# Stick-breaking attention on one core: scores and transposes as separate steps, ScalarE's norms and sigmoids in fixed groups, the mask as float32r

## The chip, the cores and the metric

The kernel runs on one core of one Trainium2 chip. The metric is the device time of one execution in microseconds (us); the kernel before has a median of 2329.46 us over 3 runs (2329.19 to 2330.55). The engines are named as in the profile: PE is TensorE, PEld its weight loads, DVE is VectorE, ACT is ScalarE, POOL is GpSimd, SP is SyncE, which issues the transfers of the weights.

## The reference, cut to what matters

A trunk of four residual layers on 512 tokens of width 1024: pooling, SSD, attention, pooling, each followed by a SwiGLU feed-forward layer. Only the third layer's mixer, the attention, is touched:

```
qkv = (h @ w_qkv).reshape(b, s, 3, 16, 64)
q = rms_norm(qkv[:, :, 0], q_norm);  k = rms_norm(qkv[:, :, 1], k_norm)
z = (q @ k.T) / sqrt(64)                       # per head, strictly causal mask
log_1m = where(mask, log_sigmoid(-z), 0)
after  = reverse cumulative sum of log_1m, without the element itself
a = where(mask, exp(log_sigmoid(z) + after), 0)
o = a @ v;   x = x + o @ w_out
```

The kernel computes the products of `1 - sigmoid(z)` directly, by a scan, and not through logarithms.

## The kernel before

Everything is kept transposed, with the model's width on the 128 partitions and the 512 tokens along a row. A projection (`proj`, `gemm`, L215 to L217) multiplies eight 128x128 weight blocks; each float32 operand is split into a float32r part and a rest, so that each block takes three matmuls of 512 columns. The weights' split (a cast on ACT at L108, a subtraction on DVE at L109) runs four pieces ahead of the matmuls that use them.

Attention works on eight pairs of heads. `ATT_STEPS`, a list of steps, gives the order in which the program is written: `p` is `pair` (two projections q and k, 48 matmuls; the norm of each; the splits of q and k per head), `v` is `values` (96 matmuls of 256 columns, for four heads), `a` is `attend`, `o` is the output projection of two pairs (48 matmuls). A scheduler then places each engine's instructions by data and buffer dependences. It may take them out of program order, but at run time each engine executes its list strictly in order.

A norm (`normal`) is a square on ACT (L781), a split of it (L220, L221), two matmuls that sum over a head's 64 rows (L246, L247), then `rsqrt`: Ln, Exp and Square on ACT (L232, L233, L235) and two steps on DVE (L236, L237). Ln and Exp need one set of ACT's tables, Sigmoid another. An instruction whose set is not loaded gets a table load ahead of it, which carries the line of that instruction. In `pair` the norms ask for no load themselves (`load=False`).

`attend` calls `head` for two heads; `head` takes three pieces of the score matrix (512, 512 and 256 columns; `PIECES`). For each piece `piece` writes z into one of the two PSUM banks `m` (L839; at L844 a matmul of an identity with `never`, both bf16, adds the mask), runs two sigmoids on ACT (c at L846, a at L847), the scan on DVE (L851) and a product (L857). `head` at once transposes the result (L875, PSUM banks `y` and `n`) and copies it to `at` (L877, ACT and DVE in turn). When both heads are done, 24 matmuls weight the values (L888) into the one bank `s`, which the norms' sums use too, and `split` writes the pair's output (two buffers with the tag `o`).

Of the kernel before, what the change touches and what calls it, by code (L numbers as in the profile page):

```python
# [3 lines left out]

# [7 lines left out]
F32R = mybir.dt.float32r  # L12
BF16 = mybir.dt.bfloat16
AF = mybir.ActivationFunctionType
# [3 lines left out]
P = 128  # L18
# [109 lines left out]
def _steps(order, **names):  # L128
    return [(names[s[0]], int(s[1:])) for s in order.split()]
# [6 lines left out]
    x="front", z="gate", d="steps", s="scan", o="out",  # L136
)

ATT_STEPS = _steps(
    "p0 p1 v0 a0 p2 v1 a1 p3 a2 v2 p4 a3 o0 p5 v3 a4 p6 a5 p7 a6 o1 a7 o2 o3",  # L140
    p="pair", v="values", a="attend", o="out",
)

SSD_BUFS = dict(u=2, state=3, f=11, a=6, w=6, o=8, c=2, d=5, sel=1)
ATT_BUFS = dict(kk=4, qq=4, ql=4, p=2, v=12, c=2, a=2, e=2, at=3, o=8)


class Trunk:
# [74 lines left out]
    def rsqrt(self, out, ss, n, load=True):  # L223

        nc = self.nc
        y, q = self.t(), self.t()
        out = y if out is None else out
        if load:
            self.tc.keep_in_program_order(
                nc.scalar.preload_act_table_set("natural_log_exp_and_others")  # L230
            )
        nc.scalar.activation(y, ss, AF.Ln, bias=self.eps, scale=1.0 / n)  # L232
        nc.scalar.activation(y, y, AF.Exp, scale=-0.5)  # L233

        nc.scalar.activation(q, y, AF.Square, scale=math.sqrt(0.5 / n))  # L235
        nc.vector.scalar_tensor_tensor(q, ss, n * EPS, q, op0=ALU.add, op1=ALU.mult)  # L236
        nc.vector.scalar_tensor_tensor(  # L237
            out, q, 1.5, y, op0=ALU.subtract, op1=ALU.mult, reverse0=True
        )
        return out  # L240
# [499 lines left out]


    def attention(self, j, nxt):
        nc = self.nc
        mm = nc.tensor.matmul
        V = nc.vector
        with self.phase("att", **ATT_BUFS) as tl:
            st = self.t((P, P))
# [5 lines left out]
            qg = tl("qg", (P, 1))  # L753
            V.tensor_scalar(qg, self.col("q_norm", 0), 1.0 / math.sqrt(HD), None, op0=ALU.mult)
            kg = self.col("k_norm", 0)
            identb = tl("identb", (P, P), BF16)
            V.tensor_copy(identb, self.ident)

            st = self.t((P, P))
            nc.gpsimd.memset(st, 0.0)  # L760
# [1 line left out]
                out=st, in_=st, pattern=[[-1, P]], base=0, channel_multiplier=1,  # L762
                compare_op=ALU.is_gt, fill=-(2.0**100),
            )
            never = tl("never", (P, P), BF16)
            V.tensor_copy(never, st)
            rcol = tl("rcol", (P, NB))
            zero = tl("zero", (P, 1))
# [4 lines left out]
            def project(q):  # L773
                ps = self.ps("g")
                self.proj(ps)
                V.tensor_tensor(q, ps, self.rstd, op=ALU.mult)
                return q

            def normal(q, gain):
                sq = self.t()  # L780
                nc.scalar.activation(sq, q, AF.Square)  # L781
                pss = self.ps("s")
                self.sums(pss, bd, sq)
                r = self.rsqrt(None, pss, HD, load=False)
                V.scalar_tensor_tensor(q, q, gain, r, op0=ALU.mult, op1=ALU.mult)

            def values(n):
# [13 lines left out]
                    vt.append(v)  # L801
                return vt

            def pair():


                q = project(tl("p"))
                k = project(tl("p"))
                normal(q, qg)
                normal(k, kg)  # L810
                heads = []
                for h in range(2):
                    own = slice(h * HD, (h + 1) * HD)
                    other = slice((1 - h) * HD, (2 - h) * HD)
                    qq, ql, kk = (tl(t, dt=F32R) for t in ("qq", "ql", "kk"))
                    nc.scalar.copy(qq[own], q[own])
                    nc.gpsimd.tensor_copy(qq[other], qq[own])
                    V.tensor_tensor(ql[own], q[own], qq[own].bitcast(F32), op=ALU.subtract)
                    nc.gpsimd.tensor_copy(ql[other], ql[own])
                    nc.scalar.copy(kk[own], k[own])  # L820
                    V.tensor_tensor(kk[other], k[own], kk[own].bitcast(F32), op=ALU.subtract)
                    heads.append((qq, ql, kk))
                return heads


            PIECES = ((0, 2), (3,), (1,))
            FIRST = {0: 0, 2: 1, 3: 4, 1: 8}

            def piece(parts, qbs):


                qq, ql, kk = parts
                n = sum(qb + 1 for qb in qbs) * P
                z = self.ps(next(zs), (P, n))
                at = 0
                for qb in qbs:
                    w = (qb + 1) * P
                    for q in (qq, ql):
                        mm(  # L839
                            z[:, at : at + w], q[:, qb * P : (qb + 1) * P], kk[:, :w],  # L840
                            start=at == 0 and q is qq, stop=False,
                        )
                    at += w
                    mm(z[:, at - P : at], identb, never, start=False, stop=qb == qbs[-1])  # L844
                c, a, e = (tl(t, (P, n)) for t in "cae")
                nc.scalar.activation(c, z, AF.Sigmoid, scale=-1.0)  # L846
                nc.scalar.activation(a, z, AF.Sigmoid)  # L847
                at = 0
                for qb in qbs:
                    w = (qb + 1) * P  # L850
                    V.tensor_tensor_scan(  # L851
                        back(e, at, w), back(c, at, w), zero.to_broadcast([P, w]), 1.0,
                        op0=ALU.mult, op1=ALU.add,
                    )
                    at += w

                V.tensor_tensor(a[:, : n - 1], a[:, : n - 1], e[:, 1:], op=ALU.mult)  # L857
                return a

            def back(t, at, n):  # L860

                (ps, pn), (s, _) = t.ap
                return bass.AP(t.tensor, t.offset + s * (at + n - 1), [[ps, pn], [-s, n]])

            copies = itertools.cycle((nc.scalar.copy, V.tensor_copy))

            def head(parts):

                at = tl("at", (P, 10, P))
                for qbs in PIECES:  # L870
                    a = piece(parts, qbs)
                    n = a.shape[1] // P
                    pt = self.ps(next(ts), (P, n, P))
                    for i in range(n):
                        nc.tensor.transpose(pt[:, i], a[:, i * P : (i + 1) * P], self.ident)  # L875
                    f = FIRST[qbs[0]]
                    next(copies)(at[:, f : f + n], pt)  # L877
                return at

            def attend(f, heads, vt):  # L880
                po = self.ps("s")
                ats = [head(heads[h]) for h in range(2)]

                todo = [(0, 0, 2), (0, 2, 4), (1, 2, 4), (2, 2, 4), (1, 1, 2), (3, 3, 4)]
                for i, (kb, lo, hi) in enumerate(todo):
                    b0, b1 = FIRST[lo] + kb, FIRST[hi - 1] + kb
                    for h in range(2):
                        mm(  # L888
                            po[h * HD : (h + 1) * HD, lo * P : hi * P].rearrange(
                                "p (b t) -> p b t", t=P  # L890
                            ),
                            vt[kb][:, (2 * f + h) * HD : (2 * f + h + 1) * HD],
                            ats[h][:, b0 : b1 + 1 : max(b1 - b0, 1)],
                            start=i == 0, stop=i == len(todo) - 1,
                        )
                hi, lo = tl("o", dt=F32R), tl("o", dt=F32R)
                self.split(po, hi, lo)
                return hi, lo
# [5 lines left out]
                    nc.tensor.transpose(pt, self.rstd[:, b * P : (b + 1) * P], self.ident)  # L904
                    V.tensor_copy(rcol[:, b : b + 1], pt[:, :1])

            qk, vals, os = {}, {}, {}
            for step, n in ATT_STEPS:
                if (step, n) == ("values", 0):
                    rstd_columns()  # L910
                if step == "values":
                    vals[n] = values(n)
                elif step == "pair":
                    qk[n] = pair()
                elif step == "attend":
                    os[n] = attend(n % 2, qk.pop(n), vals[n // 2])
                else:
                    last = n == SB_HEADS // 4 - 1
                    self.out_proj([os.pop(2 * n), os.pop(2 * n + 1)], 4, nxt, last, "ggy")
# [24 lines left out]
def _plan(subs, pool_in, pool_group, ssd_in, ssd_out, sb_qkv, sb_out, gate, up, down):  # L944
# [10 lines left out]
    for sub in subs:  # L955
# [43 lines left out]
        else:  # L999
            j = sub[2]  # L1000
            for step, n in ATT_STEPS:
                if step == "values":
# [100 lines left out]
```

## Time and profile before

| | |
|---|---|
| time of the profiled execution | 2327.25 us |
| its span (first to last instruction) | 2325.5 us |
| median of three runs | 2329.46 us |
| PE busy | 2279.9 us (98%) |
| DVE busy | 1368.6 us (59%) |
| ACT busy | 1011.4 us (43%) |
| mean granted clock of PE | 0.994 |

The span runs from the first to the last instruction; 1.75 us of the profiled execution lie around it. Busy time is the time in which an engine has an instruction running by the records; PE's ends are modelled, so that short stops between matmuls can be hidden in it. Attention takes 316.8 us of the span, from 1230.5 us (first matmul of its first projection) to 1547.3 us, where its last output projection is interleaved with the first one of the feed-forward layer.

### The profile page before, as it was taken

How to read it: one execution, taken by the hardware profiler on the slowest of the kernel's cores; microseconds unless marked ns; L12 is line 12 of the kernel's file. 1: busy time of each engine (PE TensorE's matmuls, PEld its weight loads, DVE VectorE, ACT ScalarE, POOL GpSimd, SP SyncE). 2: the span in 40 equal slices, each digit the busy share in tenths (PEclk: the TensorE clock that was granted, in tenths of full speed). 3: DMA queues.
4: the chain of work that ended last, by engine and by line, in shares of the span. 5: the costliest groups of instructions: out<-in, count | busy, mean ns of one | idle time of the engine just before them, and what ended most of it. 6: DMA issues, size and time to landing. Idle time of an engine off the chain costs nothing.

```text
span 2325.5 us, 26443 instructions
## 1 busy us (share of the span) xinstructions
PE 2279.9 (98%) x10650; PEld 1849.0 (80%) x10650; DVE 1368.6 (59%) x1889; ACT 1011.4 (43%) x1446; POOL 39.6 (2%) x132
## 2 busy tenths in 40 slices
PE   8999999999999999999999988899999999999999
PEld 7888888777777778888888766578888888888887
DVE  8744434778787785444457667884344469534443
ACT  5522223576565763222236777852222244422221
POOL 0000000000000000000001001100000000000000
PEclk9999999999999999999999989999999999999999
DMA  4323222322222223232223112022232232333231
GB/s 160 115 91 109 91 92 74 109 73 73 73 90 74 73 77 105 91 107 93 91 82 100 46 37 82 19 86 96 91 106 94 82 103 88 109 101 99 91 99 65
DMA packets 211898, 205.43 MB, mean 88 GB/s; under 512 B 4800, under 2 KB 204608, under 8 KB 211776
## 3 DMA queue, kind: packets, MB, share of 16 engines
q1 hardware_dynamic: 211632, 203.57, 27.0%
q8 instruction: 84, 1.38, 0.2%
q14 instruction: 38, 0.31, 0.0%
q10 hardware_dynamic: 144, 0.17, 0.0%
HBM read 201.63 MB, written 2.10 MB: 88 GB/s over the span
## 4 chain that ended last, share of the span: by engine, by line
PE 87%; ACT 5%; DVE 5%; issue 1%; DMA 1%; SPq 0%; POOL 0%; DVEq 0%; ACTq 0%; POOLq 0%
PE ps L215 27%; PE ps L216 27%; PE ps L217 27%; PE ps L673 1%; PE ps L888 1%; DVE e L851 1%; DVE wl L109 1%; ACT L233 1%; ACT wh L108 1%; PE ps L679 1%; ACT L232 1%; PE ps L875 0%; PE ps L642 0%; DVE a L857 0%; DMA raw<-in_pool_in_dram 0%
## 5 line engine op out<-in xcount | busy, mean ns | idle before, releaser
L108 ACT CAST wh<-raw 128x1024 fp32r<-128x1024 f32 (+3 forms) x394 | 402.7, 1023 | 1070.1 <-PE ps L216 850.1
L215 PE MATMUL ps<-xh,wh 128*128 128x512 f32 x2056 | 807.6, 394 | 5.9 <-ACT xh L261 5.9
L216 PE MATMUL ps<-xl,wh 128*128 128x512 f32 x2056 | 806.2, 392 | 0.2 <-DVE xl L262 0.2
L217 PE MATMUL ps<-xh,wl 128*128 128x512 f32 x2056 | 805.4, 392 | 0.0
L109 DVE TENSOR_TENSOR wl<-raw,wh 128x1024 fp32r<-128x1024 f32 (+3 forms) x394 | 467.6, 1187 | 71.6 <-ACT wh L108 71.1
L215 PEld LDWEIGHTS ps<-xh,wh 128*128 128x128 f32 x2056 | 386.9, 188 | 89.3 <-ACT xh L261 6.6
L216 PEld LDWEIGHTS ps<-xl,wh 128*128 128x128 f32 x2056 | 386.6, 188 | 81.9 <-DVE xl L262 1.7
L217 PEld LDWEIGHTS ps<-xh,wl 128*128 128x128 f32 x2056 | 386.6, 188 | 81.9 <-issue 2.4
L215 PE MATMUL ps<-h,wh 128*128 128x512 f32 x736 | 286.7, 390 | 0.4 <-DVE x L393 0.4
L216 PE MATMUL ps<-h,wh 128*128 128x512 f32 x736 | 286.6, 389 | 0.0
L217 PE MATMUL ps<-h,wl 128*128 128x512 f32 x736 | 286.6, 389 | 0.0
L343 DVE TENSOR_TENSOR x<-ps,x 128x512 f32<-128x512 f32 x96 | 66.4, 692 | 257.2 <-PE ps L217 257.2
L336 DVE TENSOR_TENSOR g<-ps,g 128x512 f32<-128x512 f32 x88 | 60.7, 691 | 226.3 <-PE ps L217 226.3
L327 DVE TENSOR_TENSOR g<-ps,rstd 128x512 f32<-128x512 f32 x88 | 60.6, 691 | 220.7 <-PE ps L217 220.6
L215 PEld LDWEIGHTS ps<-h,wh 128*128 128x128 f32 x736 | 138.2, 188 | 29.4 <-DVE x L393 0.8
L216 PEld LDWEIGHTS ps<-h,wh 128*128 128x128 f32 x736 | 138.2, 188 | 28.6
L217 PEld LDWEIGHTS ps<-h,wl 128*128 128x128 f32 x736 | 138.2, 188 | 28.6
L215 PE MATMUL ps<-o,wh 128*128 128x512 f32 x192 | 78.7, 410 | 2.5 <-DVE x L736 1.6
L216 PE MATMUL ps<-o,wh 128*128 128x512 f32 x192 | 78.2, 407 | 0.0
L217 PE MATMUL ps<-o,wl 128*128 128x512 f32 x192 | 77.7, 405 | 0.0
L457 DVE SCALAR_TENSOR_TENSOR c<-u,par,c 128x512 f32<-128x512 f32 x96 | 72.0, 750 | 4.1 <-ACT c L452 3.2
L330 DVE TENSOR_TENSOR g<-g,rstd 128x512 f32<-128x512 f32 x88 | 60.0, 685 | 3.2 <-ACT g L329 3.2
(190 smaller groups left out, 2077.9 us busy)
## 6 DMA issues: line engine op xcount, KB each, us to landing
raw<-in_ffn_gate_dram SPq DMA_DIRECT2D x44, 1024.0 KB, 5.0
raw<-in_ffn_up_dram SPq DMA_DIRECT2D x44, 1024.0 KB, 4.9
raw<-in_ffn_down_dram SPq DMA_DIRECT2D x32, 1024.0 KB, 4.9
raw<-in_ssd_in_dram SPq DMA_DIRECT2D x16, 1024.0 KB, 5.1
raw<-in_ffn_down_dram SPq DMA_DIRECT2D x16, 768.0 KB, 4.3
raw<-in_ssd_in_dram SPq DMA_DIRECT2D x16, 512.0 KB, 4.4
raw<-in_ssd_out_dram SPq DMA_DIRECT2D x8, 1024.0 KB, 4.9
raw<-in_sb_qkv_dram SPq DMA_DIRECT2D x16, 512.0 KB, 3.6
```

Of the source, the lines that this page charges most:

```text
L108: self.nc.scalar.copy(wh, src)
L109: self.nc.vector.tensor_tensor(wl, src, wh.bitcast(F32), op=ALU.subtract)
L215: mm(out, wh, xh, start=start and i == 0, stop=False)
L216: mm(out, wh, xl, start=False, stop=False)
L217: mm(out, wl, xh, start=False, stop=stop and i == n - 1)
L232: nc.scalar.activation(y, ss, AF.Ln, bias=self.eps, scale=1.0 / n)
L233: nc.scalar.activation(y, y, AF.Exp, scale=-0.5)
L327: nc.vector.tensor_tensor(g, ps, self.rstd, op=ALU.mult)
L330: nc.vector.tensor_tensor(sg, sg, self.rstd, op=ALU.mult)
L336: nc.vector.tensor_tensor(h, ps, h, op=ALU.mult)
L343: nc.vector.tensor_tensor(self.x[d], ps, self.x[d], op=ALU.add)
L457: V.scalar_tensor_tensor(c, u[:, k : k + SEQ], self.col("conv_w", k * nt + ch), c, op0=ALU.mult, op1=ALU.add,)
```

## The change

`attend` is cut in two. The new step `z` (`scores`) makes z, the sigmoids, the scan and the product for all six pieces of a pair and keeps the six results (tag `a`, now 7 buffers). The step `t` (`attend` with `turn`) does the transposes, the copies and the product with the values. Between a pair's `z` and its `t` stands the `p` of the pair two further on. For ACT two groups are formed: the norms of a pair begin with one table load and may be issued only behind the last sigmoid of the scores step that is written before them; the sigmoids of a scores step only behind the last Exp of the norms before them (`issue_after`, and `newest`, which holds that instruction). `identb` and `never` become float32r. Of the tiles `v`, `at` and `o` there are fewer buffers, of `c`, `a` and `e` more.

```diff
 ATT_STEPS = _steps(
-    "p0 p1 v0 a0 p2 v1 a1 p3 a2 v2 p4 a3 o0 p5 v3 a4 p6 a5 p7 a6 o1 a7 o2 o3",
-    p="pair", v="values", a="attend", o="out",
+    "p0 p1 z0 v0 p2 t0 z1 p3 t1 z2 v1 p4 t2 o0 z3 p5 t3 z4 v2 p6 t4 o1 z5 p7 t5 z6 v3 t6 z7 o2 "
+    "t7 o3",
+    p="pair", v="values", z="scores", t="attend", o="out",
 )
-ATT_BUFS = dict(kk=4, qq=4, ql=4, p=2, v=12, c=2, a=2, e=2, at=3, o=8)
+ATT_BUFS = dict(kk=4, qq=4, ql=4, p=2, v=8, c=3, a=7, e=3, at=2, o=4)
...
-        nc.scalar.activation(y, y, AF.Exp, scale=-0.5)
+        self.last_exp = nc.scalar.activation(y, y, AF.Exp, scale=-0.5).ins
...
-            identb = tl("identb", (P, P), BF16)
-            V.tensor_copy(identb, self.ident)
+            identr = tl("identr", (P, P), F32R)
+            V.tensor_copy(identr, self.ident)
...
-            never = tl("never", (P, P), BF16)
+            never = tl("never", (P, P), F32R)
...
+            newest = [None]
+
+            def behind():
+                return tc.issue_after(newest[0]) if newest[0] else nullcontext()
...
-                normal(q, qg)
-                normal(k, kg)
+                with behind():
+                    tc.keep_in_program_order(
+                        nc.scalar.preload_act_table_set("natural_log_exp_and_others")
+                    )
+                    normal(q, qg)
+                    normal(k, kg)
+                newest[0] = self.last_exp
...
-                    mm(z[:, at - P : at], identb, never, start=False, stop=qb == qbs[-1])
+                    mm(z[:, at - P : at], identr, never, start=False, stop=qb == qbs[-1])
...
-                nc.scalar.activation(a, z, AF.Sigmoid)
+                newest[0] = nc.scalar.activation(a, z, AF.Sigmoid).ins
...
-            def head(parts):
+            def scores(heads):
+                with behind():
+                    return [[piece(parts, qbs) for qbs in PIECES] for parts in heads]
+
+            def turn(pieces):
 
                 at = tl("at", (P, 10, P))
-                for qbs in PIECES:
-                    a = piece(parts, qbs)
+                for qbs, a in zip(PIECES, pieces):
...
-            def attend(f, heads, vt):
+            def attend(f, weights, vt):
                 po = self.ps("s")
-                ats = [head(heads[h]) for h in range(2)]
+                ats = [turn(pieces) for pieces in weights]
...
+                elif step == "scores":
+                    ws[n] = scores(qk.pop(n))
                 elif step == "attend":
-                    os[n] = attend(n % 2, qk.pop(n), vals[n // 2])
+                    os[n] = attend(n % 2, ws.pop(n), vals[n // 2])
```

The first place is ACT's list, where the norms of the fourth pair (p3; its tiles are `t`, an activation with `eps` is the Ln, the next one in place the Exp) meet the sigmoids of the third pair (c and a). Before:

```order
L232 ACT_TABLE_LOAD
L232 ACTIVATE t_10159<-ps_10152,eps 128x512
L846 ACT_TABLE_LOAD
L846 ACTIVATE c_10211<-ps_10204 128x512
L233 ACT_TABLE_LOAD
L233 ACTIVATE t_10159<-t_10159 128x512
L847 ACT_TABLE_LOAD
L847 ACTIVATE a_10212<-ps_10204 128x512
```

In the change the end of the norms of that fourth pair (Ln, Exp, Square of its k) and the third pair's first sigmoids (`qq` is the split of q):

```order
L234 ACTIVATE t_10011<-ps_10004,eps 128x512
L235 ACTIVATE t_10011<-t_10011 128x512
L859 ACT_TABLE_LOAD
L859 ACTIVATE c_10095<-ps_10088 128x512
L237 ACTIVATE t_10012<-t_10011 128x512
L829 CAST qq_10019<-p_9918 64x512
L829 CAST qq_10028<-p_9918 64x512
L860 ACTIVATE a_10096<-ps_10088 128x512
```

Four loads around two norm steps and two sigmoids have become one, because all sigmoids of the pair now stand behind the last Exp. In ACT's whole list there are 25 table loads fewer, all of them in the attention.

The second place is PE's list at score pieces. Before, for the third pair (`kk` with `qq` or `ql` are scores, `ident` with `a` are transposes, `t` with `bd` are the sums of a norm):

```order
L875 MATMUL ps_10219<-ident,a_10212 128x128 x4
L246 MATMUL ps_10169<-t_10170,bd_9202 128x512
L839 MATMUL ps_10258<-kk_9834,qq_9832 128x128
L839 MATMUL ps_10258<-kk_9834,ql_9833 128x128
L844 LDWEIGHTS identb_9206
L844 MATMUL ps_10258<-never_9213,identb_9206 128x128
L839 MATMUL ps_10258<-kk_9834,qq_9832 128x384
L839 MATMUL ps_10258<-kk_9834,ql_9833 128x384
L844 LDWEIGHTS identb_9206
L844 MATMUL ps_10258<-never_9213,identb_9206 128x128
L247 MATMUL ps_10169<-t_10171,bd_9202 128x512
```

In the change, for the fourth pair, the end of its third piece (`ps_10550`) to the start of its fourth (`ps_10561`); `ps_10599` is the q projection of pair p5, which is written after these scores:

```order
L218 MATMUL ps_10599<-xl_995_9025,wh_10282 128x512
L219 MATMUL ps_10599<-xh_995_9024,wl_10283 128x512
L852 MATMUL ps_10550<-kk_10021,qq_10019 128x256
L852 MATMUL ps_10550<-kk_10021,ql_10020 128x256
L857 MATMUL ps_10550<-never_9213,identr_9206 128x128
L217 MATMUL ps_10599<-xh_997_9055,wh_10282 128x512
L218 MATMUL ps_10599<-xl_997_9056,wh_10282 128x512
L219 MATMUL ps_10599<-xh_997_9055,wl_10283 128x512
L852 MATMUL ps_10561<-kk_10030,qq_10028 128x128
L852 MATMUL ps_10561<-kk_10030,ql_10029 128x128
L857 MATMUL ps_10561<-never_9213,identr_9206 128x128
```

The transposes have left this stretch. Matmuls of a later pair's projection stand between the pieces, and the separate LDWEIGHTS rows of the bf16 identity are gone.

The third place is ACT's list ahead of that pair's sigmoids (`kk` are the splits of pair p4's k; `o` is the output of the third pair, t2; `wh` is a weight piece):

```order
L833 CAST kk_10383<-p_10313 64x512
L833 CAST kk_10392<-p_10313 64x512
L222 CAST o_10446<-ps_10399 128x512
L108 CAST wh_10600<-raw_10454 128x1024
L859 ACT_TABLE_LOAD
L859 ACTIVATE c_10531<-ps_10524 128x512
L860 ACTIVATE a_10532<-ps_10524 128x512
```

With `o=4` the buffer that `o_10446` writes is the first pair's, which the output projection o0 reads to its last matmuls, and the buffer of `wh_10600` is that of o0's second weight piece; both casts stand ahead of the load and of all six pieces' sigmoids.

## Rows read from the trace of the kernel before

**Rows 1.** Stretches of the span: length, busy us of PE, PEld, DVE, ACT, POOL; clock.

```profile
1230.50:1547.30 316.80, 281.93 (x1545) 217.69 (x1544) 236.00 (x343) 227.42 (x344) 26.26 (x32) 0.96 0.18 54
1330.00:1360.00 30.00, 21.44 (x115) 16.95 (x113) 20.96 (x29) 25.52 (x37) 3.43 (x4) 0.77 0.00 1
1450.00:1505.00 55.00, 45.44 (x227) 32.38 (x226) 43.68 (x65) 47.82 (x71) 5.24 (x7) 0.99 0.08 27
1505.00:1530.00 25.00, 21.18 (x118) 14.15 (x117) 20.46 (x32) 13.61 (x24) 1.53 (x2) 0.90 0.13 43
```

**Rows 2.** Waits of PE in the attention: total us, times, longest.

```profile
PE ps L875 <- DVE a L857: 10.1, 12, 2.2
PE ps L839 <- ACT a L847: 8.8, 8, 2.7
```

**Rows 3.** ACT's timeline in the attention: start us, us, instruction.

```profile
1330.51 1.05 ACT L108 CAST wh<-raw 128x1024 fp32r<-128x1024 f32 x1 [3.04 <-PE ps L216]
...
1333.58 1.28 ACT L846 ACT_TABLE_LOAD   x1
...
1335.48 1.28 ACT L233 ACT_TABLE_LOAD   x1
...
1339.22 0.62 ACT L235 ACTIVATE t<-t 128x512 f32<-128x512 f32 x1
1339.74 0.62 ACT L781 ACTIVATE t<-p 128x512 f32<-128x512 f32 x1
```

**Rows 4.** PE's timeline, one stop in the same stretch.

```profile
1351.91 1.11 PE L888 MATMUL ps<-at,v 128*64 128x256 f32 x2 [2.89 <-DVE t L236]
```

**Rows 5.** PE's timeline where it runs without stops; starts give the pitch.

```profile
1230.53 0.39 PE L215 MATMUL ps<-xh,wh 128*128 128x512 f32 x1
...
1235.97 0.39 PE L246 MATMUL ps<-t,onesr 128*128 128x512 f32 x1
...
1293.09 0.27 PE L798 MATMUL ps<-wh,xl 128*128 128x256 f32 x1
...
1297.75 0.28 PE L798 MATMUL ps<-wh,xl 128*128 128x256 f32 x1
...
1321.06 1.26 PE L875 MATMUL ps<-ident,a 128*128 128x128 f32 x8
1322.07 0.48 PE L215 MATMUL ps<-xh,wh 128*128 128x512 f32 x1
...
1324.47 2.38 PE L888 MATMUL ps<-at,v 128*64 128x256 f32 x22
```

**Rows 6.** PE's timeline through the score piece of blocks 0 and 2.

```profile
1277.96 0.31 PE L839 MATMUL ps<-kk,qq 128*128 128x128 f32 x1
1278.10 0.28 PE L839 MATMUL ps<-kk,ql 128*128 128x128 f32 x1
1278.22 0.23 PE L844 MATMUL ps<-never,identb 128*128 128x128 bf16 x1
...
1278.69 0.23 PE L844 MATMUL ps<-never,identb 128*128 128x128 bf16 x1
1278.73 0.48 PE L216 MATMUL ps<-xl,wh 128*128 128x512 f32 x1
1279.05 0.40 PE L217 MATMUL ps<-xh,wl 128*128 128x512 f32 x1
```

**Rows 7.** Groups of the attention, by form: table loads (busy us, mean ns).

```profile
L232 ACT ACT_TABLE_LOAD x12 | 15.4, 1283 | 0.2
L233 ACT ACT_TABLE_LOAD x12 | 15.4, 1283 | 0.2
...
L846 ACT ACT_TABLE_LOAD x10 | 12.8, 1283 | 0.2
L847 ACT ACT_TABLE_LOAD x6 | 7.7, 1283 | 0.1
```

**Rows 8.** The same view: weight loads of a score block and of the mask.

```profile
L839 PEld LDWEIGHTS ps<-kk,qq 128*128 128x128 f32 x64 | 13.7, 214 | 15.9 <-ACT a L847 11.9 <-issue 3.2 <-ACT v L800 0.4
L844 PEld LDWEIGHTS <-identb 128*128 128x128 bf16 x64 | 6.6, 103 | 7.7 <-issue 6.6
```

More of the change, by code (lines that the diff above doesn't have):

```diff
@@ L2 @@
 import math
-from contextlib import ExitStack, contextmanager
+from contextlib import ExitStack, contextmanager, nullcontext
 import concourse.bass as bass
@@ L742, in attention @@
     def attention(self, j, nxt):
-        nc = self.nc
+        nc, tc = self.nc, self.tc
         mm = nc.tensor.matmul
@@ L905, in rstd_columns @@
                     V.tensor_copy(rcol[:, b : b + 1], pt[:, :1])
-            qk, vals, os = {}, {}, {}
+            qk, ws, vals, os = {}, {}, {}, {}
             for step, n in ATT_STEPS:
```

## The prediction, on record before the changed kernel was run

> **What bounds the kernel now.** I read the page's busy times first: TensorE is busy for 98% of the span, so time is to be won only where it stops or runs slowly. Then the windows of the attention, the only stage that the change touches. Of its 316.8 us TensorE is busy for 281.9 and stands still for 34.9; its mean granted clock is 0.96, and since the clock has two levels, 1.2 and 2.4 GHz, that loses 0.04 x 316.8 = 12.7 us against full speed [rows 1]. The list of waits says what it stops for: 10.1 us are transposes that wait for the product on VectorE (L857), 8.8 us scores that wait for ScalarE's second sigmoid to leave their bank (L847) [rows 2]. Both lead back to ScalarE. Its timeline shows why: a table load of 1.28 us, one step of a norm or one sigmoid, the next load [rows 3]; in the same stretch TensorE stands for 2.89 us before the product with the values [rows 4], and from 1330 to 1360 the granted clock is 0.77 [rows 1].
>
> How much could be won follows from a dense run, by the pitch from start to start where nothing stops [rows 5]. The 24 matmuls from 1230.53 to 1235.97 take 0.2267 us each: 384 of the projections, 192 of the output and 34 of the sums give 610 x 0.2267 = 138.3. The 39 matmuls of 256 columns between 1293.09 and 1297.75 take 0.1195 each: 384 x 0.1195 = 45.9. Transposes: 1.01 / 8 = 0.126, x 160 = 20.2. Weighting the values: 2.38 / 22 = 0.108, x 192 = 20.8. A score piece of 512 of a head's 1280 columns takes 1278.73 - 1277.96 = 0.77 [rows 6], a head 2.5 times that, 16 heads 30.8. The sum is 256.0 us. Attention loses 60.8: 34.9 visible stops, 12.7 of clock, and 13.2 that I can't assign (longer pitches where the form of the operands changes, stops shorter than the modelled ends).
>
> **The change, part by part.**
>
> *Table loads.* Before there are 12 + 12 + 10 + 6 = 40 of 1283 ns for norms and sigmoids [rows 7]; in the new order 15 of these are left. 25 x 1.283 = 32.1 us leave ScalarE's 227.4 busy us [rows 1]. That alone is no gain in the end time: ScalarE idles for 89 of the 316.8 us. It counts where a load stood between a norm and a sigmoid that TensorE waited for, and nearly all stops of the list are of this kind.
>
> *Scores apart from turns.* Before, the transposes of a piece stand a few matmuls behind its scores, so that two sigmoids, the scan and the product lie open on TensorE. Now 48 projection matmuls (10.9 us) lie between, and matmuls of a projection, of the values or of the output lie between the pieces. So I take the 34.9 us of stops and the 12.7 of clock away and put in what the new order has.
>
> I went through two pairs of the new order (p4 t2 o0 z3, then p5 t3 z4 v2) with the durations of the rows. (i) Behind the output projection ScalarE has to run a PSUM cast (about 0.6), a weight cast of 1.05, the load of 1.28 and two sigmoids (0.52 from start to start, 0.62 the last) [rows 3]: 4.1 us until the first score bank is free. The cast is held there by `o=4`, the weight piece by its own buffers. TensorE has two pieces (1.4) and nine projection matmuls (2.0) for that time: stops of 0.7 and, two pieces further, 0.4. (ii) The sums of q wait for VectorE's split: 0.4. (iii) Transposes use the banks y, n, y, n, y, n, and n has one buffer; the fourth and sixth piece wait until VectorE has copied the one before, between two steps of a norm: 1.7. (iv) The sums of k: 0.2. (v) Beside the values, two casts of k and the output's cast stand between the first sigmoids, and the fourth and sixth piece wait 0.6 and 0.4. Together 4.4; with signals between engines I take 5 us for two pairs, and 3.5 x 5 = 17.5 for the stage, whose first pair has no turns in its way. A first guess, not a row: each is a place where the order lets an engine come late by that much.
>
> The ends: the last scores z7 follow t6 with four pieces side by side, and t7 waits for VectorE. The stretch 1505 to 1530 of before, with the same work, has 25.0 - 21.2 = 3.8 us of stops [rows 1]; I keep it and add half for the start: 5.7. None of the new stops reaches the 2.89 us of before, so I take no loss of clock; kept at the 0.90 of 1505 to 1530 it would be 2.5 us.
>
> *What is not assigned* (13.2): fewer groups of transposes are left between float32r matmuls; I keep 10.
>
> *The mask as float32r.* Before, a mask matmul starts the next one 0.04 us later (1278.69 to 1278.73), but that one then takes 0.32 to its successor (to 1279.05) where 0.2267 is usual: 0.13 in all [rows 6]. A float32r block of 128 columns takes 0.12 (1278.10 to 1278.22). So 64 x (0.12 - 0.13), nothing. The other bound is the weight load: 214 ns for a float32r block against 103 for the bf16 identity [rows 8]; if none of the difference were hidden, 64 x 0.111 = 7.1 us more. I take nothing, since the pitch is what TensorE's end depends on.
>
> On this the Trainium skill speaks against the edit. Its page "TensorE: Matmul & The Clock Gate", in the section on weight-path perf modes, says that the fast weight load is on for 128 weights of a type that is not FP32, about twice as fast measured. The trace agrees in the load's duration (103 against 214 ns); by the rule the sum would be 7.1 us higher if the loads lay open, by the row's pitch it is unchanged.
>
> *Fewer buffers* (`v`, `at`, `o`): only `o` shows in the walk, in (i). Without the cover of the nine projection matmuls it would cost 2 us more at each of o0 and o1. The weights follow the new step order, two steps earlier or later; transfers keep their engines busy for 18% of the stage [rows 1] and stay hidden.
>
> *Sum.* 256.0 + 10 + 17.5 + 5.7 = 289.2 us, against 316.8: 27.6 less. The profiled execution would be 2327.25 - 27.6 = 2299.7; against the median of the runs, 2329.46, which lies 2.2 above it, 2301.9. I forecast 2302.
>
> **The rivals.**
>
> *VectorE becomes the bound.* Its work doesn't shrink: 236.0 busy us in the stage, 92% of TensorE's dense sum. In the long stretch where it was asked for most, 1450 to 1505, it reached 43.68 / 55 = 79% [rows 1]. If its strict order (scans ahead of the next projection's product) holds it to that, the stage takes 236.0 / 0.794 = 297 us: 19.6 less, 2310. Against it: in my walk it was late by 0.3 to 1.7 us, not by more. Chance 0.20, with results from 2309 to 2321.
>
> *The stops vanish.* With 1 us in place of 5 for two pairs, 5 unassigned and 4 at the ends: 268.5, 48 less, 2281. For it: projections, values or outputs lie between nearly all pieces. Against it: two score banks and one bank `s` for sums and outputs remain. Chance 0.13, from 2272 to 2293.
>
> *The mask's weight loads lie open*: 7.1 us on top, 2309. The fast load named above would be lost in full. The pitch of rows 6 speaks against it. Chance 0.07; from 2300 to 2316.
>
> *The gates put the engines in step* (slower). ScalarE may start no sigmoid before the norms' last Exp and no norm before the last sigmoid. If a gate opens when the cover is used up, TensorE stands for a whole group: 1.28 for the load and 12 sigmoids, about 5.4, less the 3.9 of its own scores in that time, 2.8; and for two norms of about 4 each, 8.0; 21.6 for two pairs. The point that decides is (316.8 - 256.0 - 10 - 5.7) / 3.5 = 12.9. At two thirds of 21.6, and with the clock at 0.77 as from 1330 to 1360 for a fifth of the stage (14.6), it would be 256.0 + 10 + 50.4 + 5.7 + 14.6 = 336.7, 20 more: 2349. For it: the third place of the order, where a whole chain stands ahead of z3's sigmoids. Against it: 2.8 was hidden there, and each norm has transposes, outputs or values beside it. Chance 0.06.
>
> *Nothing comes of it*: the loads leave a ScalarE that idled anyway, and the waits move to the gates, about as many: 2325 to 2334. Chance 0.04.
>
> **How the numbers follow.** Forecast (20 to 36 less, 2293 to 2309): 0.50. With the chances above the sum is 1. What a measurement of this kernel tells from no change is about 0.2%, 4.7 us: faster 0.50 + 0.20 + 0.13 + 0.07 = 0.90, same 0.04, slower 0.06. Range: below, I cut the outer half of the case without stops, 2286; above, I cut the cases of no effect and slower and the slow end of VectorE's, 2318. Within it is about 0.8; the mask's two bounds lie inside.
>
> **What would show it.** Right: 15 loads beside the one of `rstd` on ScalarE in the stage, at most 2 us for the longest stop of TensorE, 16 to 30 us of stops in all and a clock of 0.99; PE's waits led no longer by transposes behind L857's product but by score pieces behind the second sigmoid and transposes behind copies; a mask followed by matmuls at their usual pitch. Wrong: waits of whole groups behind the table loads with the clock below 0.95 (in step); VectorE above 80% with TensorE waiting for its casts and products (VectorE); a pitch over 0.2 us at the masks.

## The result and the profile after

The change takes 2293.95 us (median of 4 runs, 2292.44 to 2295.53) where before takes 2329.32 (2329.14 to 2330.55): ratio 0.9847, 95% interval 0.983 to 0.9864, 35.4 us less. The forecast was 2302 in a range from 2286 to 2318; the sum had a gain of 27.6 us, 8 less than measured. The profiled execution took 2294.82 us, its span 2293.0.

The windows of the attention in the changed kernel (first line the stage, columns as in [rows 1]; then the same in five stretches):

```profile
1232.40:1513.47 281.07, 263.84 (x1540) 216.17 (x1538) 233.12 (x339) 190.77 (x317) 25.38 (x32) 0.99 0.19 60
1232.40:1285.00 52.60, 47.48 (x247) 39.03 (x246) 40.80 (x65) 37.56 (x57) 6.37 (x8) 1.00 0.23 68
1285.00:1340.00 55.00, 48.70 (x319) 41.17 (x318) 46.62 (x68) 44.42 (x76) 6.73 (x8) 0.97 0.12 39
1340.00:1410.00 70.00, 67.90 (x401) 56.09 (x400) 60.34 (x86) 47.21 (x79) 6.14 (x8) 1.00 0.20 61
1410.00:1465.00 55.00, 53.81 (x307) 43.33 (x306) 45.53 (x64) 37.09 (x60) 6.14 (x8) 1.00 0.27 87
1465.00:1513.47 48.47, 45.95 (x275) 36.54 (x273) 39.83 (x60) 24.49 (x47) 0.00 (x0) 1.00 0.14 44
```

The stage takes 281.07 us for the 316.8 of [rows 1]: the whole gain is here. (1.4 of these 35.7 us are no gain: at the stage's end twelve matmuls of the last output projection are still to come, where before it were six. The span as a whole is 32.5 us shorter, since the stage also starts 1.9 us later in this execution.) TensorE stands still for 281.07 - 263.84 = 17.2 us (34.9 before) and loses 0.03 x 55 = 1.7 to the clock (12.7). With the dense sum of 256.0, 281.1 - 256.0 - 17.2 - 1.7 = 6.2 are not assigned (13.2). The stops lie unevenly: 5.1 + 6.3 us in the first two of the five stretches (pairs p0 to p3), 2.1 + 1.2 in the next 125 us, where the order repeats itself from pair to pair, 2.5 at the end.

TensorE's waits in the stage, as [rows 2]:

```profile
PE ps L920 <- DVE rcol L921: 3.3, 2, 2.1
PE ps L852 <- ACT a L860: 3.3, 8, 1.7
PE ps L249 <- DVE t L223: 3.0, 2, 2.8
PE ps L217 <- DVE x L738: 2.0, 3, 1.4
PE ps L904 <- DVE t L238: 1.4, 5, 0.5
```

No transpose waits for VectorE's product any longer (10.1 us in [rows 2]); scores behind the second sigmoid are down from 8.8 to 3.3. Level with these is now a wait that the prediction didn't name: the four transposes that turn `rstd` into columns (L920), each written behind VectorE's copy of the one before. In all, 11 of the 17.2 us of stops are waits for VectorE.

The table loads in the stage, answering to [rows 7]: 8 + 7 = 15 beside one for the `rstd` of the layer's norm, where there were 40.

```profile
L819 ACT ACT_TABLE_LOAD x8 | 10.3, 1283 | 0.1
L859 ACT ACT_TABLE_LOAD x7 | 9.0, 1283 | 0.1
L232 ACT ACT_TABLE_LOAD x1 | 1.3, 1283 | 0.0
```

And ScalarE's timeline at a scores step of this steady order, where [rows 3] had a load before a sigmoid and another before the Exp of a norm. One load, then twelve sigmoids without another:

```profile
1371.22 1.28 ACT L859 ACT_TABLE_LOAD   x1
1372.51 0.60 ACT L859 ACTIVATE c<-ps 128x512 f32<-128x512 f32 x1
...
1377.99 0.43 ACT L860 ACTIVATE a<-ps 128x256 f32<-128x256 f32 x1
```

The longest stop that is left, in VectorE's and in TensorE's timeline:

```profile
1313.45 0.68 DVE L864 TENSOR_TENSOR_SCAN e<-c,zero 128x256 f32<-128x256 f32 x1
1314.05 1.20 DVE L109 TENSOR_TENSOR wl<-raw,wh 128x1024 fp32r<-128x1024 f32 x1
1315.17 0.42 DVE L870 TENSOR_TENSOR a<-a,e 128x255 f32<-128x255 f32 x1
1315.50 0.68 DVE L223 TENSOR_TENSOR t<-t,t 128x512 fp32r<-128x512 f32 x1
```

```profile
1316.24 0.80 PE L249 MATMUL ps<-t,bd 128*128 128x512 f32 x1 [2.77 <-DVE t L223]
1334.04 0.50 PE L852 MATMUL ps<-kk,qq 128*128 128x512 f32 x1 [1.72 <-ACT a L860]
```

The second sum of a norm waits 2.77 us for its split (L223), which stands in VectorE's list behind the scans and products of z1 and a weight piece; from 1310 to 1320 the granted clock is 0.83, the only place in the stage where it falls.

### The profile page after: what moved, and what is told of

The parts are those of the page before. It is cut to its first block, busy times and chain, and to the rows that moved or that the text cites. A ratio compares the mean times of both kernels' runs of the same rounds, so it can differ in the third digit from the quotient of the medians.

```text
span 2293.0 us, 26394 instructions
## 1 busy us (share of the span) xinstructions
PE 2263.3 (99%) x10650; PEld 1847.7 (81%) x10650; DVE 1368.4 (60%) x1889; ACT 975.9 (43%) x1421; POOL 38.8 (2%) x132
## 4 chain that ended last, share of the span: by engine, by line
PE 87%; DVE 7%; ACT 4%; DMA 2%; issue 1%; SPq 0%; DVEq 0%; ACTq 0%
PE ps L217 27%; PE ps L218 27%; PE ps L219 27%; DVE e L864 1%; PE ps L675 1%; DVE wl L109 1%; ACT wh L108 1%; PE ps L681 1%; PE ps L644 0%; DVE ql L831 0%; DMA raw<-in_pool_in_dram 0%; DMA raw<-in_ssd_in_dram 0%; DVE a L870 0%; DVE kk L834 0%; DVE t L238 0%
```

## The experiments

Each edit is against the changed kernel unless it says so. "Stops" are the length of a stretch minus PE's busy time in it.

**The order without the gates.** Scores and turns stay apart; the norms still begin with their load, but nothing orders the groups on ScalarE.

```diff
-                return tc.issue_after(newest[0]) if newest[0] else nullcontext()
+                return nullcontext()
```

> The change without its two gates on ScalarE: steps, buffers and mask as in the change, but norms and sigmoids may mix again; its ScalarE list has 87 table loads where the change has 68 and before 93. My theory (cover and few loads both count, a load costs where TensorE waits for the bank behind it): part of the gain is lost, 2302 to 2316 us. Rival A (the table loads are all of it): 19 of 25 loads are back, so about three quarters of the 35 us are lost, 2318 to 2325. Rival B (the separate steps are all of it): as the change, 2291 to 2298.

2301.22 us, ratio 0.9875 [0.9861, 0.989]: 7.3 more than the change, 28.1 less than before, and 0.8 below the range of my theory. 34 loads stand in the stage, and the first waits are those behind norms and sigmoids; transposes wait for the product for 1.7 us in all, against 10.1 in [rows 2]:

```profile
PE ps L904 <- DVE t L238: 6.1, 5, 1.9
PE ps L852 <- ACT a L860: 5.4, 4, 4.6
...
PE ps L891 <- DVE a L870: 1.7, 2, 1.5
```

**The gates without the order.** The kernel before with the two gates alone (`attend` keeps scores and transposes together).

```diff
-                normal(q, qg)
-                normal(k, kg)
+                with behind():
+                    tc.keep_in_program_order(
+                        nc.scalar.preload_act_table_set("natural_log_exp_and_others")
+                    )
+                    normal(q, qg)
+                    normal(k, kg)
+                newest[0] = self.last_exp
...
-                ats = [head(heads[h]) for h in range(2)]
+                with behind():
+                    ats = [head(heads[h]) for h in range(2)]
```

> The kernel before with the two gates on ScalarE alone: old steps (scores and turns together), old buffers, bf16 mask, 68 table loads as in the change. My theory: the loads between norms and sigmoids are gone, but scan and product still lie open before the transposes: about half of the gain, 2306 to 2320 us. Rival A (loads alone): as the change, 2291 to 2299. Rival B (separate steps alone): as before or slower, 2326 to 2340.

2314.69 us, ratio 0.9935 [0.9921, 0.995]: 14.6 less than before, with the same 15 loads as the change, so the loads alone are not the gain. Scores wait half as long for the second sigmoid as in [rows 2], 4.5 us for 8.8, but the transposes still wait for the product, even longer:

```profile
PE ps L885 <- DVE a L867: 14.6, 15, 3.1
PE ps L849 <- ACT a L857: 4.5, 4, 2.5
```

**Turns right behind their scores.** Everything of the change except the distance between `z` and `t`; the `v` steps also stand ahead of the scores here.

```diff
-    "p0 p1 z0 v0 p2 t0 z1 p3 t1 z2 v1 p4 t2 o0 z3 p5 t3 z4 v2 p6 t4 o1 z5 p7 t5 z6 v3 t6 z7 o2 "
-    "t7 o3",
+    "p0 p1 v0 z0 t0 p2 z1 t1 p3 v1 z2 t2 o0 p4 z3 t3 p5 v2 z4 t4 o1 p6 z5 t5 p7 v3 z6 t6 o2 z7 "
+    "t7 o3",
```

> The change with another step order: each pair's turns right behind its scores (z t side by side), nothing between them; gates, buffers, mask and the 68 loads as in the change. My theory: the scan and the product lie open before the transposes again, part of the gain is lost, 2302 to 2318 us, with transposes waiting for the product in the list of waits. Rival A (loads alone): as the change, 2291 to 2298. Rival B (separate steps alone): nearly all is lost, 2318 to 2330.

2314.18 us, ratio 0.9933 [0.9916, 0.9949]: 20.2 of the 35.4 us are gone, and the time is that of the gates alone within 0.5 us. The first wait is again that of the transposes:

```profile
PE ps L891 <- DVE a L870: 15.1, 17, 1.7
```

So the distance is what takes the product's wait off TensorE; the gates alone can't. The other numbers of buffers, which this run has and the run before it has not, were never tried apart; together with the mask they show no gain at the old distance.

**Loads put back where they are covered.** One more load of the sigmoids' set ahead of each piece of 512 columns, inside the groups.

```diff
+                if qbs != (1,):
+                    tc.keep_in_program_order(
+                        nc.scalar.preload_act_table_set("sigmoid_and_others")
+                    )
```

> The change with 31 more loads of the sigmoids' own table set, one ahead of each score piece of 512 columns; no step is moved by hand, ScalarE has 40 us more to do in the stage. My theory: a load costs only where a score bank is waited for behind it; each scores step has four, partly beside projection matmuls: 10 to 25 us slower than the change, 2304 to 2319. Rival A (loads alone, each at its full price): 40 us slower, 2330 to 2336. Rival B (loads are off the path now): 2292 to 2300.

2296.31 us, ratio 0.9855 [0.984, 0.9869]: 2.4 more than the change, where I had expected 10 to 25; the total is what rival B had. 46 loads stand in the stage, 31 more than in the change:

```profile
L861 ACT ACT_TABLE_LOAD x32 | 41.1, 1283 | 0.6
```

The loads are not off the path, though. TensorE's waits at the score pieces are 7.7 us in all, 3.7 in the change (3.3 behind the second sigmoid, 0.4 without a releaser that the profile names):

```profile
PE ps L852 <- issue: 4.8, 4, 1.9
PE ps L852 <- ACT a L864: 2.9, 7, 0.6
```

At the two longest ones, 1.88 us each, ScalarE runs a load and two sigmoids, and TensorE goes on 0.1 us behind the second sigmoid. One of the two, first in ScalarE's timeline, then in TensorE's:

```profile
1399.80 1.28 ACT L861 ACT_TABLE_LOAD   x1
...
1401.58 0.59 ACT L864 ACTIVATE a<-ps 128x512 f32<-128x512 f32 x1
```

```profile
1402.28 0.30 PE L852 MATMUL ps<-kk,qq 128*128 128x128 f32 x1 [1.88 <-issue]
```

The windows up to the 25th of the 64 mask matmuls and from the 25th to the 64th (those of the change stand with the mixed masks below):

```profile
1231.72:1358.26 126.54, 120.52 (x683) 98.50 (x682) 104.62 (x154) 111.29 (x166) 13.38 (x17) 1.00 0.21 62
1358.26:1489.64 131.38, 121.14 (x729) 98.98 (x729) 109.57 (x156) 105.91 (x163) 12.67 (x16) 0.97 0.19 61
```

The ends stand at other places of the work than in the change (683 and 729 matmuls for 708 and 701), so that only stops and clock can be compared. In the second window TensorE stops for 10.2 us where the change stops for 3.7, and the clock is 0.97 for 1.00, another 3 to 4 us: about 10 us of loss, the lower end of my range. In the first it stops for 6.0 where the change stops for 12.1. About 40 of ScalarE's rows and 70 of VectorE's stand elsewhere in the lists than in the change. So the 2.4 us are a loss at the loads less a gain in the first pairs that comes with other lists; what the loads alone cost is not shown. Nor do the 7.3 us of the run without gates give the price of its 19 additional loads, since there norms and sigmoids are mixed as well.

**The mask in bf16.** `identr` and `never` as before.

```diff
-            identr = tl("identr", (P, P), F32R)
+            identr = tl("identr", (P, P), BF16)
...
-            never = tl("never", (P, P), F32R)
+            never = tl("never", (P, P), BF16)
```

> The change with the mask and its identity as bf16 again, all else as in the change. My theory (the pitch at the mask decides; in the changed kernel a float32r mask takes 0.06 and lengthens the next matmul by 0.05, together 0.11, where the bf16 one took 0.13): 64 times 0.02, so 0 to 2 us slower than the change. Rival (the loads of the weights lie open and the float32r one costs 0.11 more): 7 us faster than the change, 2285 to 2289.

2288.77 us (5 runs, 2286.55 to 2290.53), ratio 0.9829 [0.9815, 0.9842]: 5.2 faster than the change, which ran once more beside it as a control:

> The change itself once more, on the chip and in the rounds of the other kernels of this call, as what they are compared with: 2292 to 2296 us.

2293.95 (2292.7 to 2294.45). My expectation did not come true. The rival's number came true, but its mechanism is not seen. TensorE's weight loads, as [rows 8], of the mask in the change and in this version:

```profile
L857 PEld LDWEIGHTS ps<-never,identr 128*128 128x128 f32 x64 | 12.1, 189 | 0.7
```

```profile
L857 PEld LDWEIGHTS <-identr 128*128 128x128 bf16 x64 | 6.2, 96 | 7.4 <-issue 6.5
```

The load is twice as long in float32r. The pitch is not: TensorE's timeline at a mask followed by a 512-column matmul, first of the change, then of the bf16 version:

```profile
1388.53 0.22 PE L857 MATMUL ps<-never,identr 128*128 128x128 f32 x1
1388.59 0.44 PE L852 MATMUL ps<-kk,qq 128*128 128x512 f32 x1
1388.87 0.40 PE L852 MATMUL ps<-kk,ql 128*128 128x512 f32 x1
```

```profile
1368.21 0.23 PE L857 MATMUL ps<-never,identr 128*128 128x128 bf16 x1
1368.25 0.48 PE L852 MATMUL ps<-kk,qq 128*128 128x512 f32 x1
1368.57 0.39 PE L852 MATMUL ps<-kk,ql 128*128 128x512 f32 x1
```

0.06 + 0.28 = 0.34 against 0.04 + 0.32 = 0.36. Only in front of a 384-column score is bf16 the shorter, 0.30 against 0.34, sixteen times, together 0.6 us. The pitch does not hold the 5.2 us; so I made two runs with the forms mixed.

**The mask in bf16 in z0 to z2 only, and in z3 to z7 only.**

```diff
+                    mi, mn = (identb, neverb) if done[0] < 3 else (identr, never)
-                    mm(z[:, at - P : at], identr, never, start=False, stop=qb == qbs[-1])
+                    mm(z[:, at - P : at], mi, mn, start=False, stop=qb == qbs[-1])
```

> The change with the bf16 mask in the first three scores steps only (z0 to z2, 24 of the 64 mask matmuls); z3 to z7 keep the float32r mask. ScalarE's list is then the same, row for row, as with the bf16 mask everywhere, VectorE's nearly. Theory 'order' (the mask's form costs nothing by itself, it shifts where the scheduler places instructions in the first three pairs, and the 5.2 us between 2293.95 and 2288.77 come from there): 2287.5 to 2290.5, and from the 25th mask to the 64th the same stretch as in both, 117.0 us within 0.4. Theory 'price' (each float32r mask costs 5.2 / 64 = 0.08 us): 2288.8 + 40 x 0.08 = 2292.0, from 2291 to 2293.

> The other half: float32r mask in z0 to z2, bf16 in z3 to z7 (40 of 64). Theory 'order': the stretch from the 25th mask to the 64th does not get shorter than 117.0 by more than 0.4 us; the time is decided by the first three pairs, whose order here is that of neither kernel, so from 2288 to 2295; near 2294 if the stops of 2.77 and 1.72 us in the second and third pair are still there. Theory 'price': 2293.95 - 40 x 0.08 = 2290.7, with the stretch shorter by 3.2 us.

`done` counts the scores steps, `identb` and `neverb` are bf16 copies of the two tiles; the second version has `>= 3`. 2290.05 and 2290.99 us; ratios 0.9828 [0.9813, 0.9843] and 0.9833 [0.9819, 0.9848], with 2330.6 for the kernel before beside them. The windows, up to the 25th mask and from the 25th to the 64th (the steady part from here on), of the change, of bf16 everywhere, of bf16 in z0 to z2 and of bf16 in z3 to z7:

```profile
1232.40:1368.09 135.69, 123.60 (x708) 101.89 (x706) 109.23 (x162) 97.41 (x156) 15.90 (x20) 0.99 0.19 58
1368.09:1485.11 117.02, 113.31 (x701) 93.79 (x701) 102.94 (x147) 82.81 (x144) 9.48 (x12) 1.00 0.21 68
```

```profile
1230.51:1360.74 130.23, 122.03 (x707) 98.77 (x705) 108.39 (x162) 96.69 (x156) 15.82 (x20) 1.00 0.20 61
1360.74:1477.65 116.91, 113.31 (x702) 90.64 (x701) 102.96 (x148) 82.84 (x144) 9.47 (x12) 1.00 0.21 68
```

```profile
1232.31:1364.63 132.32, 123.64 (x707) 99.92 (x706) 108.73 (x164) 96.94 (x156) 15.36 (x20) 0.99 0.20 60
1364.63:1481.82 117.19, 113.33 (x700) 93.80 (x700) 102.90 (x147) 82.78 (x144) 9.47 (x12) 1.00 0.21 67
```

```profile
1230.55:1364.22 133.67, 124.00 (x707) 101.59 (x706) 109.24 (x164) 97.13 (x156) 15.82 (x20) 0.99 0.20 60
1364.22:1480.96 116.74, 113.31 (x702) 90.67 (x701) 102.95 (x148) 82.83 (x144) 9.47 (x12) 1.00 0.21 68
```

The stretch with 39 masks between its ends takes 117.02 and 117.19 us with float32r, 116.91 and 116.74 with bf16: 0.28 apart on the mean, 0.007 us a mask, half a microsecond for all 64. "Price" wanted 3.1. The bf16 in the first three pairs alone keeps nearly all of the gain, as "order" had it. The time of the second version, 2290.99, is where "price" had it too (2290.7), but not by the shorter stretch that "price" needs. The difference between the change and bf16 everywhere lies in the first three pairs: 135.69 against 130.23, in the stops (12.1 and 8.2) and in the clock, which falls once in the change (the 0.83 above) and not at all with bf16; another 0.8 lies behind the 64th mask (32.78 against 31.98). (Each window is of one execution: in the control's trace the first stretch takes 136.66 us, with stops of 11.6.) The form moves rows of the engines' lists: with bf16 about 14 of ScalarE's and 18 of VectorE's stand elsewhere, nearly all in these three pairs. In ScalarE's timeline before the 1.72 us stop shown above, the casts of k wait for a norm's last product, and behind them stand the output's cast and the sigmoids on which the score bank waits:

```profile
1331.55 1.26 ACT L833 CAST kk<-p 64x512 fp32r<-64x512 f32 x2 [1.61 <-DVE p L787]
1332.84 0.59 ACT L222 CAST o<-ps 128x512 fp32r<-128x512 f32 x1
1333.32 0.39 ACT L859 ACTIVATE c<-ps 128x256 f32<-128x256 f32 x1
```

In the bf16 version the same casts, one sigmoid earlier in the list, follow without a wait, and TensorE has no such stop. That another list moves time with the same masks is seen in the last version: in z0 to z2 they are float32r as in the change, the lists differ, and the stretch has stops of 9.7 us for 12.1, its length 133.67 for 135.69.

**The kernel before with the mask as float32r**, the same two tiles changed there.

> The kernel before with nothing but the mask as float32r (identity and never). Theory 'order': no price of its own, but the scheduler's order moves a little here too: 2329.6 within 4 us, of either sign. Theory 'price': 64 x 0.08 = 5.1 more, 2334.7; weight loads wholly open, 7.1 more, 2336.7.

2337.18 us, ratio 1.003 [1.0019, 1.0042]: 6.6 slower than the 2330.6 of the kernel before beside it, outside what "order" had allowed and where "price" with open weight loads had put it. But the time is in the stops again: from the first projection to the last output matmul 324.84 - 282.86 = 42.0 us, where the kernel before has 34.9. Answering to [rows 2]:

```profile
PE ps L875 <- DVE a L857: 17.6, 20, 2.7
PE ps L839 <- ACT a L847: 11.5, 9, 4.2
```

The pitch at its masks (0.06 + 0.28) is that of the change, and about 30 rows of ScalarE's list and as many of VectorE's stand elsewhere than in the kernel before. So the form is dear in both kernels, and in both the time is in stops and not in the masks' own pitch; whether two lists happened to come out worse, or something at a mask leads to stops that the pitch doesn't show, stays open.

**Two that changed nothing.** The four `rstd` transposes in one PSUM bank with one copy, against the 3.3 us at L920; and all copies of the transposes on ScalarE, against the waits of L891.

```diff
+                pt = self.ps("y", [P, NB, P])
                 for b in range(NB):
-                    pt = self.ps("s", [P, P])
-                    nc.tensor.transpose(pt, self.rstd[:, b * P : (b + 1) * P], self.ident)
-                    V.tensor_copy(rcol[:, b : b + 1], pt[:, :1])
+                    nc.tensor.transpose(pt[:, b], self.rstd[:, b * P : (b + 1) * P], self.ident)
+                V.tensor_copy(rcol, pt[:, :, 0])
```

> The change with the four transposes of rstd into one PSUM bank y and one copy of four columns, in place of four round trips through the single bank s. In the trace of the change TensorE waits 3.8 us for these copies. If the waits are lost time: 2 to 4 us faster than the change, 2290 to 2292. Rival (VectorE is late at this place anyway, and the wait moves to the next thing that needs it): within 1 us of the change.

```diff
-            copies = itertools.cycle((nc.scalar.copy, V.tensor_copy))
+            copies = itertools.cycle((nc.scalar.copy,))
```

> The change with all six copies of the turned weights on ScalarE, in place of three on each engine: VectorE has about 14 us less to do in the stage, ScalarE 13 more. VectorE is busy for 83% of the stage in the change, ScalarE for 68%. If VectorE's lateness is what is left on TensorE (waits for its splits, steps of norms and copies): 2 to 6 us faster, 2288 to 2292. Rival (ScalarE's chain from norm to sigmoid is what is left): 1 to 6 us slower, 2295 to 2300.

2294.94 (ratio 0.985 [0.9836, 0.9863]) and 2293.24 (0.9843 [0.9829, 0.9856]). The first is what its rival had, the second lies between its two ranges. In the first the stop moves to a transpose that waits for its copy (`PE ps L891 <- ACT at L893`, 2.6 us instead of 0.9). In the second the steady part is 3.3 us shorter, 1.5 of it in stops (2.2 for 3.7) and the rest in busy time, as five fewer matmuls stand in it; the first stretch is 3.3 longer (138.96 us). Sums of norms now wait 4.4 us for ScalarE:

```profile
1370.22:1483.96 113.74, 111.55 (x696) 92.34 (x695) 94.89 (x133) 87.37 (x155) 9.47 (x12) 1.00 0.20 65
```

**The three together**: bf16 mask, copies on ScalarE, one copy of the `rstd` columns.

> The best version by the runs so far: the change with the bf16 mask everywhere, all copies of the transposes on ScalarE, and the four rstd transposes in one PSUM bank with one copy. Added up from the runs with one of them each (5.2, 0.7 and -1.0 less): 2289; if the one rstd copy takes away the stop of 2.5 us that the bf16 version has there, 2286. From 2284 to 2291.

2286.74 us (4 runs, 2286.51 to 2287.8), ratio 0.9814 [0.98, 0.9829]: the best version, not told apart by its interval from the bf16 mask alone, and below the change and the kernel before. Its stops up to the 25th mask are 8.3 us and from there to the 64th 1.4, where the bf16 mask alone has 8.2 and 3.6.

## Why the prediction was right, and where it was off

*Right.* The time fell, by the mechanism named. The wait of the transposes for the product is gone, and turning at once brings 15.1 us of such waits and 20.2 us of time back. The loads number 15. The clock is at 0.99. The two parts are not additive: gates alone 14.6 (with the bf16 mask and the old buffers), order alone 28.1 (with the new ones), both 35.4, so 7.3 of the gates' gain is left once the order has its own. That a load counts where TensorE waits behind it was step one of the working; the run with more loads shows the one half, longer waits at score pieces behind loads, and neither run shows what a load without a waiter costs.

*The terms.* Forecast 256.0 + 10 + 17.5 + 5.7 = 289.2; measured 256.0 + 6.2 + 17.2 + 1.7 = 281.1. What failed is the size of "5 us for two pairs". In the 117 us with the scores of five pairs TensorE stops for 3.7 us, 0.7 a pair for my 2.5. The places are those of the walk, at a fraction of the price: (i) 0.19 for 1.1, beside a stop of 0.32 at the output projection, which waits for VectorE and is not in the walk; (iii) 0.46 for 1.7; (v) 0.27 and 0.18 for 1.0; at (ii) and (iv) none above 0.15. Most of what I counted did not appear; that matmuls which the scheduler placed between covered it is the likely reason, and no run shows it apart. The opposite error stands at the start: "whose first pair has no turns in its way" passed over the first three pairs, where the columns of `rstd` and the norms meet a full VectorE. They stop for 12.1 us, half of it in three stops of 2.77, 2.15 and 1.13 at which the walk never looked. The ends' 5.7 came out as 2.5 at the last one. "At most 2 us for the longest stop" was wrong by 2.77 and 2.15, and "no loss of clock" by 1.7: that a stop shorter than the 2.89 us of before leaves the clock alone did not hold for the 2.77. Of the unassigned 10, 6.2 were there. That the total came within 8 us is in part luck: for the five pairs the walk had 12.5 us of stops and 3.7 came, for the pairs ahead of them and the start it had 5 + 1.9 and 12.1 came.

*The mask* was priced at nothing, by pitch, and by pitch it is nearly nothing (0.5 us in all). As a part of the change it takes back 5.2 us, and the sign "a mask followed by matmuls at their usual pitch" did not come (0.28 for 0.2267): the step that failed is "the pitch is what TensorE's end depends on". In the steady part the pitch was the right price, but the form also changes the lists around it, which no row of before can show; that these make the whole 5.2 us is borne out by where the time lies, and not shown by a run with both forms on one list. The Trainium skill's page "TensorE: Matmul & The Clock Gate", section on weight-path perf modes, holds for the duration (96 against 189 ns); in these runs the difference is hidden, since the stretch with 39 masks differs by 0.28 us.

*The rivals.* VectorE is not the bound of the stage (233.1 / 281.07 = 83%), but it is near it in the steady part, 102.94 of 117.02 us, 88%, so the 79% that the rival took for its pace was no ceiling; with copies taken off it the stops there fall from 3.7 to 2.2 us, though the list changes there too. So the sign named for this rival, VectorE above 80% with TensorE waiting for it, did come, with 11 of the 17.2 us of stops, but not its price: the stage is not held to VectorE's pace. The gates never held TensorE for a whole group: the longest wait of scores is 1.72 us.

## What to carry to other kernels

Count a table load, or any step off the bounding engine, by who waits right behind it, and read the answer stretch by stretch: 31 extra loads cost 2.4 us in all, but that was 6.5 us more of stops in the later pairs, most of it at score pieces, with a lower clock, and 6.1 us less in the first ones, where the lists had come out otherwise. Put a chain through three engines (scores, sigmoid, scan and product, transpose) a whole projection apart, before its links are made faster. Where a scheduler writes the lists, compare them before a run even for an edit that seems only to change a type, and test such an edit apart from the rest.

## What the runs showed of the hardware that I had not expected

A mask is paid for in the instruction behind it, and in either form: the next 512-column matmul takes 0.32 us to its successor behind a bf16 mask and 0.28 behind a float32r one, where 0.2267 is usual [rows 5], and the mask itself only 0.04 or 0.06. (In front of a 384-column matmul the float32r mask takes 0.11 itself.) In float32r the operands don't change form there, so the change of form, which the prediction had among the unassigned time, is not the whole reason.

A table load was followed by its activation at once: 1371.22 to 1372.51 is 1.29 us from start to start. The Trainium skill's page "ScalarE: Activation LUTs", section "What ACT_TABLE_LOAD costs", gives 2.66 us for a switch of sets, with a drain; the trace shows no such second part here.
